# The first block's transitions of a fused transformer kernel: four weight tiles of the next stage are multiplied with the unnormalized residual sum, and the layer norm is applied to the products

## Chip, cores and metric

The kernel runs on one core of one Trainium2 chip. The metric is the device time of one execution in microseconds; lower is better. Three timed runs and one profiled execution of the kernel before are shown.

## What is computed

The input is one sequence of 256 tokens with 1024 features, in float32. The first block has two layers (the second block follows and is not touched). In each layer a mixer (sparse attention in layer 0, differential attention in layer 1) and a squared-ReLU MLP of 4096 hidden units are added to the stream through a layer norm:

```python
for l in range(DEPTH):
    sh1, sc1, g1, sh2, sc2, g2 = split(c_act @ ada_w[l] + ada_b[l], 6)
    y = mixer(modulate(x, sh1, sc1))
    x = layer_norm(ALPHA * x + (1 + g1) * y, ln_g[l, 0], ln_b[l, 0])
    y = sq_relu_mlp(modulate(x, sh2, sc2))
    x = layer_norm(ALPHA * x + (1 + g2) * y, ln_g[l, 1], ln_b[l, 1])
# modulate(x, shift, scale) = x * (1 + scale) + shift
```

A layer norm followed by `modulate` is `(r - mu) * rs * a + b` for each token, with a mean `mu` and an inverse deviation `rs` per token and a scale `a` and a shift `b` per feature. A following projection with weights `W` is therefore `rs * (W.(a*r) - mu * W.a) + W.b`: the product with the unnormalized `a*r` can be made before `mu` and `rs` are known.

## The kernel before

Activations lie with features on the partitions and the 256 tokens along the row, as eight tiles of 128x256. Every number that is multiplied is split into a high half in the reduced float32 format of TensorE (`fp32r`) and a low half, the rest; `mm3` (L385) makes three matmuls of 128x128 by 128x256 for each product: high by high, high by low, low by high. The stream is in `xa`, the modulated input of the next stage in `hh` (high halves) and `hl` (low halves).

All weights come from memory as tiles of 128x1024, 512 KB each (`load_raw`, L333, on the SP queue, whose order is that of the program). ScalarE makes the high half (`cast_hi`, L346, or L365 in `fetch`), VectorE or GpSimd the low half (`cast_lo`, L349, or L366). One tile of `up` or of a projection is 24 matmuls into one PSUM bank, one tile of `down` is 24 matmuls that add to eight output tiles `y` in four banks.

A transition is `tail` (L702) with `ln_finish` (L613) and `mod_apply` (L653). `tail` takes the last weight tiles of the stage that ends (`held`), loads the first eight tiles of the stage that follows (`following`), casts the first four of them, and finishes the output tiles one by one in the order 0, 2, 4, 6, 1, 3, 5, 7. For each, `tile_` (L626) adds gate times output to the stream (L633, VectorE), squares it (L635, ScalarE) and adds up sums and squares (L548: VectorE and GpSimd); narrow matmuls with ones make the column sums (L543). `rstd_rows` (L578) makes mean and variance on VectorE, the power of -0.5 on GpSimd (L591), and broadcasts both along the partitions into PSUM by eight small matmuls (L575). `warm` (L596) puts matmuls with zeros between. Then `apply` (L665) goes through the eight tiles: subtract the mean (L669), scale (L673), high half with the shift (L609, ScalarE), low half (L611). After the loop come the residual updates for the next transition (L515).

The transitions that the diff touches:

- Transition 1, `rest0` (L1505): the output projection of layer 0 into the first MLP. Right after it `late_loads` (L1914) loads the constants of the later stages, behind a GpSimd copy (L437) that reads the last tile of `hh`.
- Transition 2, the end of the first `mlp` (L833) into layer 1, `mix1` (L1532). The work list there is `ORDER1` (L33): eight value tiles, then `q` and `k` of eight heads; `queue1` (L1589) starts a head of attention when the values and its `q` and `k` are there. VectorE, ScalarE and GpSimd work in the program's order there.
- Transition 3, `rest1` (L1687): the output projection of layer 1 into the second MLP. Before that MLP two GpSimd operations (L1702, L1703) make a copy of the second block's meta tokens.

The stage that follows transitions 1 and 3 begins with `mlp_head` (L820): the first four `up` tiles, with the tiles' eight row slices outermost, so that it can start when the first tile of `hh` is there. In `mlp` the dot products of later modulation vectors (`ada`, L491: a 512 KB load and one VectorE operation each) and then the residual updates are spread over the loop by `tick` (L511).

Outside of regions marked `manual_schedule` (SP everywhere; TensorE in `tail`, by the last entry of `MAN`, L38), a scheduler fixes each engine's order when the program is built: among what is ready in its own estimate, what comes first in the program. `fenced` (L371) keeps weight casts on ScalarE and VectorE behind the last operations of `apply` on the same engine.

## Time and profile before

| | |
|---|---|
| median of three runs | 1179.38 us (1176.38 to 1181.78) |
| profiled execution | 1184.45 us |
| its span, first to last instruction | 1182.7 us |
| granted TensorE clock, mean | 0.942 |
| transition 1, 2, 3: last down matmul ends at | 219.87, 411.70, 555.67 us |
| first matmul with the new `hh` | 226.19, 418.76, 569.17 us |

Times inside the profiled execution count from the start of its span. A line of the timeline gives the start, the duration, the engine, the line of the program, the operation, the tile written and the tiles read, how many were merged, and in brackets how long the engine was idle before and what ended that. Matmuls overlap, so a duration of 0.28 us stands for a step of about 0.12 us from start to start.

### The profile page before, as it was taken

The numbers are of one execution on the slowest core, as the hardware profiler recorded it, in microseconds if no ns is written. First come the engines' busy times: TensorE is split into PE (matmuls) and PEld (weight loads), VectorE is DVE, ScalarE is ACT, GpSimd is POOL, SyncE is SP. The second block draws the span as 40 slices with busy tenths as digits, with TensorE's granted clock in tenths as the row PEclk, the third lists the DMA queues.
The fourth block names the chain that finished last, engine by engine and source line by source line (L and its number), as shares of the span: only waits on it lengthen the run. The fifth ranks groups of instructions, "written<-read, shape, count | busy, mean of one in ns | idle before, by whom it ended". The sixth has DMA issues, their size and how long they took to land.

```text
span 1182.7 us, 20550 instructions
## 1 busy us (share of the span) xinstructions
PE 1088.2 (92%) x7766; PEld 989.8 (84%) x7766; DVE 836.4 (71%) x1656; ACT 603.8 (51%) x1256; POOL 313.5 (27%) x343
## 2 busy tenths in 40 slices
PE   2889989999999999887999999998799989999997
PEld 1768667999999978777999999897786888899996
DVE  7575986799886577766886555579996667755553
ACT  2455757464445456554654444467445353644442
POOL 3283563200000208665000000417654350000000
PEclk9786998999999989898899999899999997999999
DMA  9966642299996238446387554022211151756520
GB/s 344 313 253 208 250 166 82 104 388 345 340 334 230 90 114 279 146 159 232 118 309 251 189 185 140 12 86 93 73 54 37 72 193 45 267 191 184 190 90 36
DMA packets 60448, 212.59 MB, mean 180 GB/s; under 512 B 6619, under 2 KB 9084, under 8 KB 60348
## 3 DMA queue, kind: packets, MB, share of 16 engines
q1 hardware_dynamic: 59424, 209.43, 50.9%
q0 software_dynamic: 192, 0.79, 0.4%
q8 instruction: 61, 1.00, 0.4%
q10 hardware_dynamic: 732, 1.05, 0.3%
q14 instruction: 39, 0.32, 0.1%
HBM read 209.15 MB, written 1.84 MB: 178 GB/s over the span
## 4 chain that ended last, share of the span: by engine, by line
PE 69%; DVE 13%; DMA 5%; POOL 5%; issue 4%; ACT 3%; SPq 0%; POOLq 0%; DVEq 0%; ACTq 0%
PE y L387 10%; PE y L388 10%; PE y L389 10%; PE pj L387 7%; PE pj L388 7%; PE pj L389 7%; PE tr L392 3%; DMA raw<-in_ws 3%; PE y L401 2%; DVE lo L352 2%; PE y L392 1%; PE pj L392 1%; DVE cva L2176 1%; PE cm L392 1%; DVE raw L478 1%
## 5 line engine op out<-in xcount | busy, mean ns | idle before, releaser
L366 DVE TENSOR_TENSOR lo<-raw,hi 128x1024 fp32r<-128x1024 f32 (+1 forms) x208 | 226.8, 1106 | 107.0 <-ACT hi L365 106.9
L365 ACT ACTIVATE hi<-raw 128x1024 fp32r<-128x1024 f32 (+1 forms) x208 | 195.3, 958 | 94.7 <-PE pj L388 77.0
L387 PE MATMUL pj<-hh,hi 128*128 128x256 f32 x768 | 217.1, 283 | 0.3
L388 PE MATMUL pj<-hl,hi 128*128 128x256 f32 x768 | 216.6, 282 | 0.3 <-DVE hl L1749 0.3
L389 PE MATMUL pj<-hh,lo 128*128 128x256 f32 x768 | 215.7, 281 | 0.0
L352 POOL TENSOR_TENSOR lo<-raw,hi 128x512 fp32r<-128x512 f32 (+3 forms) x48 | 75.4, 1577 | 360.6 <-ACT hi L347 355.1
L352 DVE TENSOR_TENSOR lo<-raw,hi 128x1024 fp32r<-128x1024 f32 (+2 forms) x103 | 124.0, 1211 | 41.8 <-ACT hi L347 40.5
L387 PEld LDWEIGHTS pj<-hh,hi 128*128 128x128 f32 x768 | 145.1, 189 | 2.7 <-ACT relu L807 0.9
L388 PEld LDWEIGHTS pj<-hl,hi 128*128 128x128 f32 x768 | 145.1, 189 | 2.0 <-DVE hl L1749 0.5
L388 PE MATMUL y<-actl,hi 128*128 128x256 f32 x512 | 144.3, 282 | 1.3 <-DVE actl L810 1.2
L389 PEld LDWEIGHTS pj<-hh,lo 128*128 128x128 f32 x768 | 145.3, 189 | 0.0
L387 PE MATMUL y<-acth,hi 128*128 128x256 f32 x512 | 144.1, 281 | 0.0
L389 PE MATMUL y<-acth,lo 128*128 128x256 f32 x512 | 143.7, 281 | 0.0
L347 ACT ACTIVATE hi<-raw 128x1024 fp32r<-128x1024 f32 (+2 forms) x107 | 110.7, 1042 | 24.1 <-DMA raw<-in_ws 13.7
L388 PEld LDWEIGHTS y<-actl,hi 128*128 128x128 f32 x512 | 97.0, 189 | 1.9 <-DVE actl L810 1.9
L387 PEld LDWEIGHTS y<-acth,hi 128*128 128x128 f32 x512 | 97.1, 190 | 0.1
L389 PEld LDWEIGHTS y<-acth,lo 128*128 128x128 f32 x512 | 96.8, 189 | 0.0
L478 DVE CUSTOM_DVE_ANT_0 raw<-raw,cact 128x1024 f32<-128x1024 f32 x67 | 86.6, 1301 | 3.3 <-DMA raw<-in_ws 3.1
L388 PE MATMUL y<-hl,hi 128*128 128x256 f32 x296 | 86.6, 293 | 0.0
L387 PE MATMUL y<-hh,hi 128*128 128x256 f32 x264 | 81.5, 309 | 2.2 <-ACT f L1586 2.2
L809 ACT ACTIVATE acth<-act 128x256 fp32r<-128x256 f32 x96 | 39.4, 416 | 83.5 <-DVE act L808 83.5
L389 PE MATMUL y<-hh,lo 128*128 128x256 f32 x264 | 77.9, 295 | 0.0
(658 smaller groups left out, 2556.9 us busy)
## 6 DMA issues: line engine op xcount, KB each, us to landing
raw<-in_ws SPq DMA_DIRECT2D x372, 512.0 KB, 4.7
bm<-bscr SPq DMA_DIRECT2D x4, 512.0 KB, 14.2
raw<-in_ws SPq DMA_DIRECT2D x4, 416.0 KB, 8.8
bm<-in_ws SPq DMA_DIRECT2D x3, 512.0 KB, 8.5
raw<-in_ws SPq DMA_DIRECT2D x3, 408.0 KB, 3.8
zn<-in_ws SPq DMA_DIRECT2D x2, 512.0 KB, 6.9
xa<-in_xT SPq DMA_DIRECT2D x2, 512.0 KB, 6.9
oh<-in_ws SPq DMA_DIRECT2D x2, 512.0 KB, 7.8
```

The lines of the kernel that those rows point to most:

```text
L347: return self.nc.scalar.activation(w[1], w[0], AF.Copy)
L352: return eng.tensor_tensor(w[2][:, a:b], w[0][:, a:b], w[1][:, a:b].bitcast(F32), op=OP.subtract)
L365: i = nc.scalar.activation(hi[:, a:b], raw[:, a:b], AF.Copy)
L366: j = (lo_by or nc.vector).tensor_tensor(lo[:, a:b], raw[:, a:b], hi[:, a:b].bitcast(F32), op=OP.subtract)
L387: mm(out, lh, rh, start=start, stop=False, skip_group_check=True)
L388: mm(out, lh, rl, start=False, stop=False, skip_group_check=True)
L389: mm(out, ll, rh, start=False, stop=stop, skip_group_check=True)
L392: self.nc.tensor.matmul(out, l, r, start=start, stop=stop, skip_group_check=True)
L401: last = self.nc.tensor.matmul(out, l, r, start=start, stop=stop, skip_group_check=True)
L478: nc.vector.tensor_tensor_reduce(out=raw, in0=raw, in1=self.cact, op0=OP.mult, op1=OP.add, scale=0.5, scalar=0.0, accum_out=t)
L809: nc.scalar.activation(ah, f, AF.Copy)
L2176: nc.vector.scalar_tensor_tensor(a, x[:, i:i + 272], w[:, j, i:i + 1], a, op0=OP.mult, op1=OP.add)
```

## The change

In the three transitions the first four weight tiles that follow (the head) are multiplied with `a*r`, whose high and low halves go into `hh` and `hl` as the output tiles are finished (`raw`). Two more columns, 256 and 257, hold `a` and `b`, so the same matmuls (258 columns) also make `W.a` and `W.b`. The head takes the two `pj` banks and `y0` and `y1`; its eight steps are put between the column sums and the broadcasts of mean and scale, whose rows now go to `y2` and `y3`; the fillers are gone there. `apply` still makes the normalized `hh` and `hl`, in the order `KS`, in the place of the raw ones, for the later weight tiles. Each head is read out of PSUM by `head_value`: two columns copied by ScalarE, `mu * W.a - product` and a multiplication by `rs` on VectorE; then `head_act` (activation of the MLP) or `head_qk` (scaled copy). The first is placed in the sixth step of the loop, three behind it.

In transition 2 the head is q0, k0, q1, k1, which `ORDER1` no longer has, and the eight tiles loaded ahead are these and v0 to v3. In the MLPs a fifth and sixth tile (`up4`, `dn0`) are cast in the transition, their low halves on GpSimd, the fourth tile's low half moves to GpSimd too, GpSimd is put into the program's order in `tail`, the downs of the first four tiles follow one by one between the next ups, and the meta-token copies are emitted among the dot products of the second MLP.

```diff
-ORDER1 = """v0 v1 v2 v3 v4 v5 v6 v7 q0 k0 q1 k1 q2 k2 q3 k3 q4 k4 q5 k5 q6 k6 q7 k7"""
+ORDER1 = """v0 v1 v2 v3 v4 v5 v6 v7 q2 k2 q3 k3 q4 k4 q5 k5 q6 k6 q7 k7"""
...
+            if head:
+                c.mod.raw(m, r[m])
             if n == 7:
                 c.one[1]()
                 c.two[1]()
-                self.warm(2)
+                if head:
+                    next(head)
+                else:
+                    self.warm(2)
                 c.one[1]()
                 c.two[1]()
...
+            st = self.ln_stats(c.s)
+            next(head)
+            mu = self.rows_of(st[:, 0:2], "y2")
             next(work, None)
-            c.mod(c.r, mu, rs, work)
+            next(head)
+            rs = self.rows_of(st[:, 2:4], "y3")
+            for _ in head:
+                pass
+            c.mod.apply(c.r, mu, rs, work, evict)
...
+        def raw(m, r):
+            hh, hl = self.hh[:, m, 0:256], self.hl[:, m, 0:256]
+            nc.scalar.activation(hh, r, AF.Copy, scale=c.a[:, m:m + 1])
+            nc.vector.scalar_tensor_tensor(hl, r, c.a[:, m:m + 1], hh.bitcast(F32), op0=OP.mult, op1=OP.subtract)
...
+            for n in range(10):
+                if n < 8:
+                    m = KS[n]
+                    nc.vector.tensor_sub(r[m], r[m], mu)
+                if n == 1:
+                    nc.scalar.activation(rows, rs, AF.Copy)
+                    nc.scalar.activation(mus, mu, AF.Copy)
+                if 1 <= n < 9:
+                    k = KS[n - 1]
...
+                if n == 5:
+                    evict(0, mus, rows)
+            self.fence = [self.fence_, lo()]
+            for j in range(1, 4):
+                evict(j, mus, rows)
...
+    def raw_head(self, ws):
+        ps = self.heads = [self.PS(t) for t in ("pj", "pj", "y0", "y1")]
+        for n, k in enumerate(KS):
+            sl = slice(128 * k, 128 * k + 128)
+            for p, (wh, wl) in zip(ps, ws):
+                self.mm3(p[:, :258], wh[:, sl], wl[:, sl], self.hh[:, k, 0:258], self.hl[:, k, 0:258], n == 0, n == 7)
+            yield
+
+    def head_value(self, j, mu, rs):
+        nc = self.nc
+        p = self.heads[j]
+        ab = self.T(self.small, (128, 2), "headab", bufs=4)
+        nc.scalar.activation(ab, p[:, 256:258], AF.Copy)
+        t = self.T(self.lnp, (128, 256), "full", bufs=3)
+        nc.vector.scalar_tensor_tensor(t, mu, ab[:, 0:1], p[:, 0:256], op0=OP.mult, op1=OP.subtract)
+        nc.vector.tensor_mul(t, t, rs)
+        return t, ab[:, 1:2]
...
-        with self.ordered(MAN[4]):
+        with self.ordered("PG" if evict else MAN[4]):
...
+            if evict:
+                self.cast_lo(nx[2], nc.vector)
+                self.cast_hi(nx[3])
+                self.cast_lo(nx[3], nc.gpsimd)
 
             def work():
+                if evict:
+                    for n in following[4:6]:
+                        w = self.arrive(n)
+                        self.cast_hi(w)
+                        more.append(w)
+                    yield
+                    for w in more:
+                        self.cast_lo(w, nc.gpsimd)
+                    yield
+                    return
...
+    def head_act(self, j, mu, rs):
+        t, b = self.head_value(j, mu, rs)
+        self.pend.append((j, self.mlp_act(t, scale=-1.0, bias=b)))
...
-        return [f"up{l}_{j}" for j in range(5)] + [f"dn{l}_{j}" for j in range(3)]
+        return [f"up{l}_{j}" for j in range(5)] + [f"dn{l}_0"] + ([f"up{l}_5", f"dn{l}_1"] if l < 2 else
+                                                              [f"dn{l}_1", f"dn{l}_2"])
...
-        n = 8 * len(vectors) + 8
+        self.fill = self.chain(*(self.ada(*lv) for lv in vectors), more, self.fill)
+        n = 8 * len(vectors) + 10
...
-            while len(pend) > 1 and pend[0][0] < 29:
+            while len(pend) > (4 if j < 8 else 1) and pend[0][0] < 29:
...
-            with self.fenced():
-                nc.gpsimd.tensor_copy(mh, meta)
-                nc.gpsimd.tensor_tensor(ml, meta, mh.bitcast(F32), op=OP.subtract)
...
+    def meta_eight(self):
+        nc = self.nc
+        self.mrep = [self.T(self.acts, (128, 8, 128), tag, F32R) for tag in ("oh", "ol")]
+        mh, ml = (t.rearrange("p k (e t) -> p k e t", e=8) for t in self.mrep)
+        meta = self.metaT[:, :, None, :].to_broadcast([128, 8, 8, 16])
+        nc.gpsimd.tensor_copy(mh, meta)
+        yield
+        nc.gpsimd.tensor_tensor(ml, meta, mh.bitcast(F32), op=OP.subtract)
```

## Rows read from the trace of the kernel before

**Rows 1.** Part 4 of the page: the chain that ended last, shares of the span by engine.

```profile
PE 69%; DVE 13%; DMA 5%; POOL 5%; issue 4%; ACT 3%; SPq 0%; POOLq 0%; DVEq 0%; ACTq 0%
```

**Rows 2.** Windows: stretch, busy us of five engines, clock, DMA share, GB/s.

```profile
219.87:226.19 6.32, 6.31 (x37) 4.66 (x35) 2.93 (x10) 0.93 (x2) 1.23 (x2) 0.73 0.01 4
411.70:418.76 7.06, 6.86 (x33) 4.91 (x32) 3.24 (x11) 1.22 (x3) 1.26 (x2) 0.63 0.00 0
555.67:569.17 13.50, 8.62 (x33) 6.45 (x33) 7.98 (x14) 1.22 (x3) 6.47 (x5) 0.50 0.24 91
242.62:400.00 157.38, 157.38 (x1330) 157.38 (x1331) 128.26 (x196) 79.12 (x122) 2.40 (x1) 1.00 0.85 310
```

**Rows 3.** Timeline of transition 1, all engines; the last row from TensorE's own timeline.

```profile
220.07 0.48 DVE L633 SCALAR_TENSOR_TENSOR zn<-y,mod,xa 128x256 f32<-128x256 f32 x1 [0.43 <-PE y L389]
...
222.32 0.16 DVE L585 TENSOR_SCALAR st<-tr 128x2 f32<-128x2 f32 x1 [1.76 <-PE tr L392]
...
222.53 2.41 PE L392 MATMUL y<-p_first,st 128*128 128x128 f32 x8
...
222.95 0.72 POOL L591 TENSOR_TENSOR st<-va,mhalf 128x2 f32<-128x2 f32 x1 [2.57 <-DVE va L587]
...
224.98 0.48 DVE L673 SCALAR_TENSOR_TENSOR full<-zn,acol,y 128x256 f32<-128x256 f32 x1 [0.37 <-PE y L392]
...
226.19 0.47 PE L387 MATMUL pj<-hh,hi 128*128 128x256 f32 x1
...
242.62 0.39 PE L388 MATMUL y<-actl,hi 128*128 128x256 f32 x1 [1.21 <-DVE actl L810]
```

**Rows 4.** Windows: the head of the first MLP, four up tiles.

```profile
226.19:237.81 11.62, 11.62 (x97) 11.34 (x96) 11.44 (x27) 7.80 (x17) 0.50 (x2) 1.00 0.25 86
```

**Rows 5.** Timeline of VectorE in transition 1: one step of the loop.

```profile
228.74 0.41 DVE L669 TENSOR_TENSOR zn<-zn,y 128x256 f32<-128x256 f32 x1
229.07 0.47 DVE L673 SCALAR_TENSOR_TENSOR full<-zn,acol,y 128x256 f32<-128x256 f32 x1
229.46 0.48 DVE L611 SCALAR_TENSOR_TENSOR hl<-full,bcol,hh 128x256 fp32r<-128x256 f32 x1
229.86 0.41 DVE L669 TENSOR_TENSOR zn<-zn,y 128x256 f32<-128x256 f32 x1
```

**Rows 6.** Timeline of VectorE and GpSimd ahead of transition 1: casts alone and together.

```profile
206.45 1.22 DVE L352 TENSOR_TENSOR lo<-raw,hi 128x1024 fp32r<-128x1024 f32 x1
...
207.51 2.44 POOL L352 TENSOR_TENSOR lo<-raw,hi 128x1024 fp32r<-128x1024 f32 x1 [13.05 <-ACT hi L347]
...
208.85 2.19 DVE L352 TENSOR_TENSOR lo<-raw,hi 128x1024 fp32r<-128x1024 f32 x1 [1.18 <-ACT hi L347]
```

**Rows 7.** Timeline of GpSimd and SP behind transition 1; landing of the transfer issued at 236.49.

```profile
233.17 0.18 POOL L437 COPY p_late<-hh 128x1 f32<-128x1 f32 x1 [9.51 <-ACT hh L609]
...
236.49 0.87 SPq L336 DMA_DIRECT2D raw<-in_ws  x2
...
DMA to landing us min/median/max: 11.1/11.1/11.1
```

**Rows 8.** Windows: values of layer 1; its first four projections; the other twelve.

```profile
418.76:442.30 23.54, 23.54 (x100) 18.87 (x99) 17.97 (x34) 14.06 (x25) 0.00 (x0) 0.96 0.36 122
442.30:454.70 12.40, 12.40 (x106) 11.93 (x105) 9.35 (x19) 8.58 (x20) 12.08 (x8) 1.00 0.91 335
454.70:521.00 66.30, 56.72 (x422) 50.51 (x420) 47.75 (x113) 41.50 (x123) 48.69 (x42) 0.92 0.59 197
```

**Rows 9.** Timeline of GpSimd and TensorE in transition 3.

```profile
555.75 1.04 POOL L1702 CAST oh<-metaT 128x1024 fp32r<-128x1024 f32 x1 [1.98 <-PE y L389]
...
557.61 2.77 POOL L1703 TENSOR_TENSOR ol<-metaT,oh 128x1024 fp32r<-128x1024 f32 x1
...
561.56 1.01 PE L392 MATMUL tr<-ones,run 128*128 128x1 f32 x4 [3.44 <-POOL run L559]
```

**Rows 10.** Timeline of VectorE behind the loop of transition 1.

```profile
233.56 0.87 DVE L519 SCALAR_TENSOR_TENSOR xa<-zn,lnalpha,hfull 128x256 f32<-128x256 f32 x2
```

More of the change, by code (lines that the diff above doesn't have):

```diff
@@ L23 @@
 W2 = 4
+KS = (0, 2, 4, 6, 1, 3, 5, 7)
 UNIT = 2
@@ L653, in mod_apply @@
     def mod_apply(self, li, sc, sh):
         nc = self.nc
+        c = SimpleNamespace()
         def begin():
             sc1, shift = self.need(*sc), self.need(*sh)
-            a = self.T(self.small, (128, 8), "acol", bufs=2)
-            b = self.T(self.small, (128, 8), "bcol", bufs=2)
-            nc.vector.tensor_mul(a, sc1, self.lncol[:, 2 * li, :])
-            nc.vector.tensor_mul(b, sc1, self.lncol[:, 2 * li + 1, :])
-            nc.vector.tensor_add(b, b, shift)
-            def apply(r, mu, rs, work):
-                lo = None
-                for m in range(10):
-                    if m < 8:
-                        nc.vector.tensor_sub(r[m], r[m], mu)
-                    if 1 <= m < 9:
-                        k = m - 1
-                        full = self.T(self.lnp, (128, 256), "full", bufs=3)
-                        nc.vector.scalar_tensor_tensor(full, r[k], a[:, k:k + 1], rs, op0=OP.mult, op1=OP.mult)
-                        if lo:
-                            lo()
-                        lo = self.put(k, full, b[:, k:k + 1])
-                    if m == 2:
-                        next(work, None)
-                self.fence = [self.fence_, lo()]
-                rows = self.T(self.resid, (128, 1024), "hfull", bufs=1)[:, :256]
-                nc.scalar.activation(rows, rs, AF.Copy)
-                self.fill = self.residual(li, r, rows)
@@ new lines, in apply @@
+        def apply(r, mu, rs, work, evict):
+            rows = self.T(self.resid, (128, 1024), "hfull", bufs=1)
+            rows, mus = rows[:, 0:256], rows[:, 256:512]
+            lo = None
+            for n in range(10):
[7 more added lines that the diff above has]
+                    k = KS[n - 1]
+                    full = self.T(self.lnp, (128, 256), "full", bufs=3)
+                    nc.vector.scalar_tensor_tensor(full, r[k], c.a[:, k:k + 1], rs, op0=OP.mult, op1=OP.mult)
+                    if lo:
+                        lo()
+                    lo = self.put(k, full, c.b[:, k:k + 1])
+                if n == 2:
+                    next(work, None)
+                if n == 5:
[3 more added lines that the diff above has]
+                evict(j, mus, rows)
+            self.fill = self.residual(li, r, rows)
@@ L714, in tail @@
             acts = before()
-            self.idle = self.PS("pj")
+            if not evict:
+                self.idle = self.PS("pj")
             if acts is not None:
@@ L729, in work @@
                     yield
-            for n, m in enumerate((0, 2, 4, 6, 1, 3, 5, 7)):
+            head = (self.raw_head([w[1:] for w in nx]),) if evict else ()
+            for n, m in enumerate(KS):
                 if m > 3:
@@ L737, in tail @@
                 self.down(y, m, (wh, wl), *a, last=True)
-                finish[1](n, m, y[m])
-                if n == 3:
+                finish[1](n, m, y[m], *head)
+                if n == 3 and not evict:
                     for w in nx[3:]:
@@ L742, in tail @@
             k = work()
-            self.warm(1)
-            finish[2](k)
+            if not evict:
+                self.warm(1)
+            finish[2](k, *head, *((evict,) if evict else ()))
             for _ in k:
                 pass
-        for n, w in zip(following, nx):
+        if evict:
+            nx = []
+        for n, w in [*zip(following, nx), *zip(following[4:], more)]:
             self.done[n] = w[1], w[2]
@@ L797, in out_proj, with mlp_act @@
         finish[0]()
-        self.tail(self.y, [(f"{name}{k}", halves(k)) for k in order], finish, following)
+        self.tail(self.y, [(f"{name}{k}", halves(k)) for k in order], finish, following, evict=evict)
         self.y = []
-    def mlp_act(self, p):
+    def mlp_act(self, p, **affine):
         nc = self.nc
```

94 lines of the change are left out of this document (62 added, 32 removed).

## Prediction

> **What bounds the kernel now.** I read the page first: TensorE holds 69% of the chain that ended last and VectorE 13% [rows 1], so time can be won where TensorE waits or does filler, and VectorE is the next to bind. Then the windows around the three places that the diff touches, from the end of the last down matmul to the first useful matmul of what follows: 6.32 us (transition 1, into the first MLP), 7.06 us (transition 2, into layer 1) and 13.50 us (transition 3, into the second MLP) [rows 2]. TensorE reads as busy there, but on zeros, sums and row broadcasts, at 0.50 to 0.73 of its clock. The last row of the group shows what stands behind transition 1: 157.38 of 157.38 us busy, so what is won before it stays won unless weights come late. The timeline of transition 1 says what fills the gap: last residual sum 220.07, statistics 222.32, power on GpSimd until 223.67, row broadcasts from 222.53, first scaled tile 224.98, head 226.19; and one more stall of 1.21 us at 242.62 [rows 3]. All three gaps together are 26.9 us.
>
> **The change, part by part.** The head (four weight tiles in eight slices each, 96 matmuls) no longer waits for the statistics. It took 11.62 us [rows 4]: 0.121 us for a matmul, 1.45 us for each of its eight k steps, 2.9 us for a weight tile of 24 matmuls; 258 columns for 256 add under 0.1 us. Removed: 8 filler matmuls per transition, off the path once real work stands there. Added on VectorE: 8 low halves of the raw sum before the statistics, and per head one correction and one multiply. One step of the normalizing loop, 1.12 us, is a subtraction (0.33 us from start to start), a scaling (0.39) and a low half (0.40) [rows 5]. So 8 x 0.40 = 3.2 us are added before the statistics and 4 x (0.40 + 0.33) = 2.9 us behind the head. Off VectorE go the casts of one to three weights (1.22 us each [rows 6]), to GpSimd. ScalarE gets 8 high halves, four copies of two columns and a row copy; it waits for VectorE through these stretches, so I cost it at nothing; without that cover it is 8 x 0.5 us.
>
> **Transition 1.** VectorE was idle before the last sum and before the statistics [rows 3], so of the 3.2 us I put 1.0 us on the path: statistics at 223.3. TensorE meanwhile does k step 1, then the sums, k step 2, the mean rows, k step 3, the scale rows, in an order that is fixed: subtraction from about 225.6, scaling from 227.9, head done at 235.0 (219.87 + 8 x 1.45 + 3.5: the eight row broadcasts took 2.41 us at about half the clock [rows 2, 3], so 1.2; the narrow sums, which lay between 220.07 and 222.32, I estimate at 1.2; 1.1 for one wait for VectorE). The loop's subtractions are done early, so 8 x 0.79 us end at about 235.5, held at the end by the head, which still reads what is overwritten. The evictions follow, one bank each 0.73 us; up-tile 4 needs the first bank and runs 236.0 to 238.9, and the downs need all four banks and the first activation: 239.0 against 242.62 [rows 3]. That is 3.6 us won.
>
> It is given back by the weights. The constants and all later loads wait on SP behind a GpSimd copy of the last normalized tile (233.17); the up-tile issued as the seventh transfer, at 236.49, landed 11.1 us later, at 247.6 [rows 7], 14.4 us after that copy. Now the copy comes at about 235.9, and the seventh transfer is up-tile 6: landed 250.3, cast 251.4. TensorE, which does up 4 before 239.0 and then down 0, up 5 and down 1, wants it at 239.0 + 3 x 2.9 = 247.7 and gets it at 251.4; before, it had done the same number of tiles at 242.6 + 3 x 2.9 = 251.3. Sum for transition 1: 0. Bounds: 3.6 us gain if the weights are in time, 4 us loss if the loop ends 4 us later.
>
> **Transition 2.** By the same sum the head (q0, k0, q1, k1) ends 15.1 us after the last down (411.7): 426.8. The values need the head's banks, evicted in order, so I start them at 428.3; they took 23.54 us at a clock of 0.96, some of it low, so 22.6: 450.9. Before, values and these four projections were done at 454.7 [rows 8]: 3.8 us won. What follows (454.7 to 521: 56.7 of 66.3 us busy [rows 8]) waits between heads of attention. The first scores now start about 2 us later, the second and third earlier. I add nothing for that; bounds 3 us loss to 10 us gain, since these waits move with the order on four engines. The transfers are the same eight, in another order.
>
> **Transition 3.** Here two GpSimd operations of the next stage, 1.04 and 2.77 us, ran between the sums of squares, and TensorE waited 3.44 us for the last one [rows 9]. The change emits them later, inside the MLP; but it also puts a weight cast of some 2.4 us ahead of the sums on the same engine [rows 6]. I let the head start at 557.5 (last down 555.67), give it 11.6 us, 3.5 us for sums, rows and a wait, 2 us for the clock, which was 0.50 through this gap [rows 2], and 2 us for GpSimd: done at 576.6 against about 581.2 (569.17 + 11.6 and a first part at half clock), 4.6 us won, less 1 us for the evictions in front of the downs: 3.6 us. No constants are loaded here, and weights can start early, since two of them are cast at once. Bounds: 0 to 10 us.
>
> **Sum.** 0 + 3.8 + 3.6 = 7.4 us off the profiled execution of 1184.45 us (span 1182.7): 1177.0. That execution lies 5.1 us above the median of the runs, 1179.38; against the median the forecast is 1172.0 us.
>
> **Rivals.**
> (a) The gaps come back in full: weights in time in transition 1 (3.6), attention of layer 1 moving ahead with its first heads (8), transition 3 down to the pattern of transition 1 (10, its bound): 21.6 us, 1158. For it: TensorE is never without work that is ready. Against: every evicted bank and every overwritten tile goes through VectorE, already without a gap in the loop [rows 5].
> (b) It moves and doesn't shrink, or the change doesn't do what it says: the scheduler pulls the two GpSimd operations forward again. That it does such things is in the trace: a residual update that is emitted behind 32 dot products of the MLP ran at 233.56, right behind the loop [rows 10]. The weights bind in transition 1, the banks in transition 2: about 1179, within 2 us.
> (c) Slower: VectorE and GpSimd shut each other out. Place: GpSimd's casts behind the power (two more, 2.44 us each), beside the loop's and the raw sum's low halves. Rows: a cast that takes VectorE 1.22 us took 2.19 us beside one of 2.44 us on GpSimd and ended 1.1 us after it [rows 6]. Price: up to 4.9 us in each transition, with 3.2 and 2.9 us of new work all on the path: 11 us against the 6.3 and 7.1 us of gaps 1 and 2, and level in gap 3; that is 4.7 + 3.9 = 8.6 us slower, 1188. It decides from the point where the loop ends more than about 3 us later than the head. Against it: the casts beside the loop are two per transition, and only low halves were seen to stop beside one. The Trainium skill, page SBUF — State Buffer, section Who interferes with whom, states it as a rule: a VectorE instruction with two inputs in SBUF and a GpSimd instruction that reads SBUF exclude each other for the whole instruction. By that rule (the trace agrees in this pair) subtraction and scaling, which read one input from PSUM, go on, about half of the 4.9 us is lost in each of the three transitions, and the sum would be about 1179 instead of 1172.
>
> **Numbers.** A measurement of this kernel can tell about 0.5%, 5.9 us, from no change. Forecast (gain of 4 to 11 us) 0.50; (a) 0.12; (b) 0.22; (c) 0.16. Faster by over 5.9 us: (a) and most of the forecast, 0.43, together 0.55. Same: (b) and the rest of the forecast, 0.29. Slower: (c), 0.16. The forecast's own range is 1168 to 1176. With 2 in 10 left out, the lower half of (a) and the upper part of (c), the range is 1159 to 1185.
>
> **What would show it.** Right: matmuls of 258 columns directly behind the last down in all three transitions at full clock; in transition 1 a stall of TensorE for up-tile 6 near 248; the values' start near 428 held by an eviction; no wait for a sum of squares over 1 us in transition 3. Wrong: no such stall and the MLP running 3 us earlier; VectorE low halves of over 1 us beside GpSimd casts; the two GpSimd operations again in front of the power; attention of layer 1 ending more than 8 us earlier or later against the values' end. If any one transition loses more than 3 us, or layer 1's attention shifts by 8, the forecast falls.

## The result and the profile after

The changed kernel takes 1213.15 us (median of four runs, 1209.84 to 1215.45) against 1178.1 us of the kernel before: ratio 1.0291, 95% interval 1.0255 to 1.0327. The forecast was 1172, with a range of 1159 to 1185: wrong in sign. The profiled execution has a span of 1213.7 us (before 1182.7).

To see where 31 us went, I took the starts of the first residual sums (`zn<-y,mod,xa`, one row per transition in the view of the tile `zn`) as marks. The row has the shortest, median and longest of eight operations in ns, then the start of the first and of the last.

```profile
L635 DVE SCALAR_TENSOR_TENSOR zn<-y,mod,xa x8: 468/472/485, 211.5 to 217.7; 128x256 f32<-128x256 f32 x8
L635 DVE SCALAR_TENSOR_TENSOR zn<-y,mod,xa x8: 469/476/485, 419.4 to 425.6; 128x256 f32<-128x256 f32 x8
L635 DVE SCALAR_TENSOR_TENSOR zn<-y,mod,xa x8: 470/473/477, 570.2 to 586.9; 128x256 f32<-128x256 f32 x8
L635 DVE SCALAR_TENSOR_TENSOR zn<-y,mod,xa x8: 472/481/484, 770.3 to 776.6; 128x256 f32<-128x256 f32 x8
```

From mark to mark come four stretches and a rest; T4 is the last transition of the first block, which the change leaves alone. All runs of this study, in us (median of the timed runs; ratio to the kernel before; then the stretches of the profiled execution):

| run | median | ratio, interval | to T1 | T1 to T2 | T2 to T3 | T3 to T4 | rest |
|---|---|---|---|---|---|---|---|
| before | 1178.1 | | 214.1 | 191.4 | 141.4 | 200.4 | 435.4 |
| **after** | 1213.15 | 1.0291 (1.0255-1.0327) | 211.5 | 207.9 | 150.8 | 200.1 | 443.4 |
| t1_only | 1191.44 | 1.0123 (1.0085-1.0162) | 207.6 | 206.2 | 140.3 | 200.2 | 433.1 |
| t2_only | 1191.37 | 1.0148 (1.0082-1.0214) | 207.9 | 192.3 | 147.8 | 200.7 | 438.3 |
| t3_only | 1181.40 | 1.0038 (1.0011-1.0065) | 208.0 | 191.6 | 142.2 | 201.8 | 436.2 |
| rr_bank | 1211.40 | 1.0300 (1.0249-1.0351) | 208.3 | 207.7 | 150.4 | 200.3 | 441.0 |
| steps_first | 1197.05 | 1.0160 (1.0109-1.0211) | 207.7 | 202.9 | 140.5 | 203.7 | 437.2 |
| fillers | 1205.04 | 1.0225 (1.0201-1.0249) | 209.3 | 204.5 | 143.9 | 203.4 | 443.1 |
| no_raw_low | 1205.36 | 1.0225 (1.0197-1.0254) | 209.4 | 204.2 | 146.8 | 201.5 | 443.4 |
| gate_first | 1210.17 | 1.0269 (1.0226-1.0313) | 210.3 | 203.5 | 151.3 | 200.4 | 443.3 |
| ticks_late | 1200.25 | 1.0188 (1.0134-1.0241) | 205.4 | 197.6 | 146.8 | 203.3 | 444.2 |
| before_ticks | 1178.75 | 0.9991 (0.9973-1.0009) | 209.5 | 191.1 | 141.3 | 200.4 | 435.3 |
| casts_off | 1218.91 | 1.0351 (1.0300-1.0402) | 207.1 | 203.8 | 154.7 | 210.3 | 439.3 |
| meta_after | 1210.71 | 1.0281 (1.0250-1.0312) | 210.8 | 207.8 | 150.3 | 201.7 | 442.2 |
| all_five | 1184.18 | 1.0054 (1.0025-1.0084) | 208.6 | 192.5 | 142.8 | 199.0 | 437.6 |
| two_three | 1184.17 | 1.0065 (1.0035-1.0095) | - | - | - | - | - |
| five_no_low | 1180.99 | 1.0027 (0.9999-1.0055) | 207.2 | 192.2 | 140.9 | 201.0 | 437.9 |
| four_mends | 1184.80 | 1.0043 (1.0014-1.0073) | 210.3 | 192.2 | 143.2 | 200.0 | 436.4 |
| six_mends | 1181.68 | 1.0026 (1.0007-1.0045) | 207.4 | 190.5 | 143.8 | 198.8 | 434.7 |

The profiled execution of two_three lay 16 us above its median, so its stretches are left out. The first column, where no kernel differs in the work, spreads over 9 us, the rest over some 3 us in kernels that have the same code there: smaller differences in one execution are not read.

After against before: -2.6, +16.5, +9.4, -0.3, +8.0, together the 31.0 us. So transition 1 with its MLP loses most, transition 2 next, transition 3 nothing; and 8 us are lost in the second block, which the diff doesn't touch.

**Transition 1, the statistics.** Timelines of VectorE, of TensorE and of GpSimd in the changed kernel:

```profile
217.72 0.47 DVE L635 SCALAR_TENSOR_TENSOR zn<-y,mod,xa 128x256 f32<-128x256 f32 x1
218.11 1.89 DVE L702 SCALAR_TENSOR_TENSOR hl<-zn,abcol,hh 128x256 fp32r<-128x256 f32 x2
219.92 0.41 DVE L561 TENSOR_TENSOR run<-run,zn 128x256 f32<-128x256 f32 x1
220.26 0.87 DVE L702 SCALAR_TENSOR_TENSOR hl<-zn,abcol,hh 128x256 fp32r<-128x256 f32 x2
226.58 0.16 DVE L677 TENSOR_SCALAR st<-tr 128x2 f32<-128x2 f32 x1 [5.45 <-PE tr L394]
229.99 0.75 DVE L711 TENSOR_TENSOR zn<-zn,y 128x256 f32<-128x256 f32 x2 [2.86 <-PE y L394]
...
220.39 1.87 PE L394 MATMUL tr<-ones,run 128*128 128x1 f32 x8 [2.61 <-DVE run L561]
222.12 0.56 PE L389 MATMUL pj<-hh,hi 128*128 128x258 f32 x1
...
224.84 0.85 PE L394 MATMUL tr<-ones,zn 128*128 128x1 f32 x4
...
218.12 0.73 POOL L558 TENSOR_TENSOR run<-sq,sq 128x256 f32<-128x256 f32 x1 [1.73 <-ACT sq L637]
218.93 0.79 POOL L561 TENSOR_TENSOR run<-run,sq 128x256 f32<-128x256 f32 x1
```

Two raw low halves stand ahead of the last running sum on VectorE and take 1.89 us; running sums of squares run on GpSimd beside them (218.12 to 219.72). The next two, with GpSimd idle, take 0.87 us. TensorE, whose order is fixed, waits 2.61 us for that sum; then its clock is at half, and the head's first step takes 2.7 us (222.12 to 224.84), not 1.45. The statistics come 8.9 us after the last residual sum (217.72 to 226.58); before, 2.25 [rows 3]. The windows show what that does to VectorE; five after and five before, in the same places counted from the transition (columns as in [rows 2]: behind the length of the stretch stand the busy times of PE, PEld and VectorE):

```profile
217.78:222.78 5.00, 2.39 (x11) 2.39 (x12) 3.35 (x7) 3.02 (x7) 1.51 (x2) 0.65 0.02 5
222.78:227.78 5.00, 5.00 (x25) 5.00 (x25) 0.48 (x3) 0.00 (x0) 0.57 (x1) 0.50 0.00 0
227.78:232.78 5.00, 5.00 (x37) 5.00 (x36) 2.28 (x7) 0.77 (x2) 4.83 (x3) 0.82 0.00 0
247.78:252.78 5.00, 2.43 (x19) 2.02 (x17) 4.59 (x10) 0.85 (x4) 1.52 (x2) 1.00 1.03 416
252.78:257.78 5.00, 3.42 (x14) 3.12 (x15) 5.00 (x11) 1.83 (x4) 0.00 (x0) 0.57 1.04 404
```

```profile
219.87:224.87 5.00, 4.99 (x32) 4.21 (x31) 1.72 (x6) 0.42 (x1) 1.23 (x2) 0.76 0.01 3
224.87:229.87 5.00, 5.00 (x34) 3.84 (x33) 4.89 (x14) 2.33 (x5) 0.00 (x0) 0.90 0.01 2
229.87:234.87 5.00, 5.00 (x44) 5.00 (x44) 4.82 (x13) 3.50 (x9) 0.50 (x2) 1.00 0.09 18
249.87:254.87 5.00, 5.00 (x46) 5.00 (x45) 5.00 (x10) 1.80 (x4) 0.00 (x0) 1.00 1.03 419
254.87:259.87 5.00, 5.00 (x45) 5.00 (x44) 5.00 (x10) 4.14 (x8) 0.00 (x0) 1.00 1.03 415
```

In the first 15 us VectorE works 6.11 us after and 11.43 us before: 5.3 us of it are lost waiting for statistics, while it has more to do. TensorE pays 30 us later. **The stall in the MLP**, VectorE, TensorE and ScalarE:

```profile
250.37 0.68 DVE L368 TENSOR_TENSOR lo<-raw,hi 128x512 fp32r<-128x512 f32 x1
250.97 1.22 DVE L480 CUSTOM_DVE_ANT_0 raw<-raw,cact 128x1024 f32<-128x1024 f32 x1
252.12 1.23 DVE L480 CUSTOM_DVE_ANT_0 raw<-raw,cact 128x1024 f32<-128x1024 f32 x1
...
251.11 0.39 PE L391 MATMUL pj<-hh,lo 128*128 128x256 f32 x1 [2.34 <-DVE lo L368]
...
254.35 0.58 PE L391 MATMUL y<-acth,lo 128*128 128x256 f32 x1 [1.79 <-DVE lo L368]
...
241.40 2.18 ACT L367 ACTIVATE hi<-raw 128x512 fp32r<-128x512 f32 x4
```

The weights lay in SBUF (ScalarE made their high halves from 241.4 to 243.6); the four low halves that belong to them are made at 245.35, 250.37, 253.61 and 255.70. The second stands on VectorE behind the loop, the evictions and the late constants (1.02 us of it an idle wait for their transfer), the third behind two dot products more (L480).

**Transition 2** has the same picture (first row), and ahead of it a new shut-out: an activation's square on VectorE takes 2.49 us beside the fourth tile's cast on GpSimd (415.13 to 417.57). **Transition 3**: the two copies of the meta tokens still run between the sums of squares (the three POOL rows). **Block 2** begins with a wait for a PSUM bank:

```profile
428.31 1.87 PE L394 MATMUL tr<-ones,run 128*128 128x1 f32 x8 [2.72 <-DVE run L561]
...
415.35 2.49 DVE L895 TENSOR_TENSOR act<-relu 128x256 f32<-128x256 f32 x1 [0.80 <-ACT relu L894]
...
582.18 1.23 POOL L1812 CAST oh<-metaT 128x1024 fp32r<-128x1024 f32 x1 [2.26 <-PE y L391]
583.49 2.39 POOL L1814 TENSOR_TENSOR ol<-metaT,oh 128x1024 fp32r<-128x1024 f32 x1
585.84 0.90 POOL L558 TENSOR_TENSOR run<-sq,sq 128x256 f32<-128x256 f32 x1
...
797.43 0.57 PE L389 MATMUL a<-hi,oh 128*128 128x272 f32 x1 [2.17 <-DVE full L1887]
```

### The profile page after: what moved, and what is told of

It is laid out like the page before. It is cut to its first block, busy times and chain, and to the rows that moved or that the text cites. A ratio compares the mean times of both kernels' runs of the same rounds, so it can differ in the third digit from the quotient of the medians.

```text
span 1213.7 us, 20617 instructions
## 1 busy us (share of the span) xinstructions
PE 1095.1 (90%) x7742; PEld 999.9 (82%) x7742; DVE 852.5 (70%) x1697; ACT 618.0 (51%) x1298; POOL 333.1 (27%) x350
## 4 chain that ended last, share of the span: by engine, by line
PE 65%; DVE 16%; DMA 5%; issue 5%; POOL 4%; ACT 4%; POOLq 0%; DVEq 0%; SPq 0%; ACTq 0%
PE y L389 10%; PE y L391 10%; PE y L390 9%; PE pj L389 7%; PE pj L391 7%; PE pj L390 7%; PE tr L394 3%; DVE lo L354 3%; DMA raw<-in_ws 3%; PE y L403 2%; DVE raw L480 1%; PE y L394 1%; DVE cva L2284 1%; PE d L394 1%; POOL se L1557 1%
## 5 line engine op out<-in xcount | busy, mean ns | idle before, releaser
L368 DVE TENSOR_TENSOR lo<-raw,hi 128x1024 fp32r<-128x1024 f32 (+1 forms) x204 | 221.3, 1102 | 101.1 <-ACT hi L367 100.8
L367 ACT ACTIVATE hi<-raw 128x1024 fp32r<-128x1024 f32 (+1 forms) x204 | 190.6, 955 | 89.3 <-PE pj L390 70.3
L391 PE MATMUL pj<-hh,lo 128*128 128x256 f32 (+1 forms) x752 | 214.2, 285 | 4.5 <-DVE lo L368 4.5
L389 PE MATMUL pj<-hh,hi 128*128 128x256 f32 (+1 forms) x752 | 215.5, 287 | 0.2 <-ACT hh L1856 0.2
L390 PE MATMUL pj<-hl,hi 128*128 128x256 f32 (+1 forms) x752 | 214.9, 286 | 0.7 <-DVE hl L613 0.3
L354 POOL TENSOR_TENSOR lo<-raw,hi 128x512 fp32r<-128x512 f32 (+3 forms) x55 | 94.6, 1727 | 390.7 <-ACT hi L349 377.2
L354 DVE TENSOR_TENSOR lo<-raw,hi 128x1024 fp32r<-128x1024 f32 (+2 forms) x95 | 119.0, 1259 | 49.2 <-ACT hi L349 46.6
L349 ACT ACTIVATE hi<-raw 128x1024 fp32r<-128x1024 f32 (+2 forms) x111 | 115.0, 1042 | 36.0 <-DMA raw<-in_ws 15.1
L390 PE MATMUL y<-hl,hi 128*128 128x256 f32 (+1 forms) x312 | 90.6, 291 | 0.0
L389 PE MATMUL y<-hh,hi 128*128 128x256 f32 (+1 forms) x280 | 85.8, 307 | 3.4 <-ACT f L1688 1.8
L480 DVE CUSTOM_DVE_ANT_0 raw<-raw,cact 128x1024 f32<-128x1024 f32 x67 | 86.3, 1292 | 3.4 <-DMA raw<-in_ws 3.4
L391 PE MATMUL y<-hh,lo 128*128 128x256 f32 (+1 forms) x280 | 82.7, 295 | 0.0
```

Of the source, the lines that this page charges most:

```text
L349: return self.nc.scalar.activation(w[1], w[0], AF.Copy)
L354: return eng.tensor_tensor(w[2][:, a:b], w[0][:, a:b], w[1][:, a:b].bitcast(F32), op=OP.subtract)
L367: i = nc.scalar.activation(hi[:, a:b], raw[:, a:b], AF.Copy)
L368: j = (lo_by or nc.vector).tensor_tensor(lo[:, a:b], raw[:, a:b], hi[:, a:b].bitcast(F32), op=OP.subtract)
L389: mm(out, lh, rh, start=start, stop=False, skip_group_check=True)
L390: mm(out, lh, rl, start=False, stop=False, skip_group_check=True)
```

## Experiments

### One transition at a time

Edit: for the transitions left as before, the old functions are called (`mod_apply`, `mlp_first`, `mlp_head`, `ORDER1` and the place of the meta copies of the kernel before).

> Only transition 1 is changed; transitions 2 and 3 are those of the kernel before. From the two traces: the changed kernel's first residual sum of transition 2 comes 13.8 us later than before although transition 1 began 2.6 us earlier, so transition 1 and the MLP behind it lose 16.4 us by themselves. Theory A (each transition loses for itself): about 13 to 16 us slower than before (1191 to 1194), and in block 2 no further loss. Rival (one shared cause, the shift of the weight stream after transition 1, makes all the losses): the whole 31 us, 1209.

> Only transition 2 is changed. Theory A: 9.5 us lost between the first residual sums of transitions 2 and 3, and 4.7 us at the start of block 2, where the first product that goes into bank a has to wait 2.2 us for the last normalizing product of VectorE, which reads the rows from the same physical bank in the changed program and from another one in the program before; together 14 us slower (1192), 17 if the half clock near 901 us comes with it. Rival (shared cause): within 3 us of before, 1178.

> Only transition 3 and the two GpSimd copies of the meta tokens are changed. Theory A: level with before (0.3 us faster in the changed kernel's trace), 1178, and no wait for bank a at the start of block 2. Rival 1 (its gain is eaten by the late state that the earlier transitions leave): 3 to 4 us faster, 1175, as predicted. Rival 2 (the loss in block 2 belongs to the moved copies): 8 us slower, 1186.

Measured: +1.23%, +1.48%, +0.38%, together 3.1% against 2.9% for all three. Transitions 1 and 2 lose for themselves, and no shared cause carries the losses on; transition 3 alone is within 0.5% of level. Transition 2 alone also lengthens the start of block 2: from T4's first residual sum to block 2's first `xp` it is 39.1 us, with transition 1 alone 35.8, before 36.0, after 41.2.

### Order of TensorE, clock, and the raw low halves

```diff
             if n == 7:
+                if head:
+                    next(head)
+                    next(head)
                 c.one[1]()
                 c.two[1]()
-                if head:
-                    next(head)
-                else:
+                if not head:
                     self.warm(2)
```

> The changed kernel with another order on TensorE: the head's first two steps stand ahead of the column sums of the last tiles, instead of one step between them. In the changed kernel TensorE waits 2.61 us for a running sum that VectorE makes behind two low halves of the raw sum, its clock falls to half, and the statistics come 8.8 us after the last down matmul (before: 2.5). Theory A (this late start is the larger part of transition 1's loss): no wait over 1 us there, statistics 3 to 5 us earlier in all three transitions, 6 to 12 us faster than the changed kernel, 1202 to 1207. Rival V (VectorE's own amount of work sets the end, whenever the statistics come): under 3 us faster.

Measured: 16 us faster than after. In transitions 1 and 2 there is no wait and a clock of 1.00; the statistics come 4.7 us after the last residual sum (213.9 to 218.59 in transition 1). T1 to T2 gives back 5.0 us, T2 to T3 10.3, all that transition 2 had lost. Not so in transition 3: TensorE waits 3.53 us for a residual sum, its clock is 0.50 before and behind that wait, and T3 to T4 is 3.6 us longer. Theory A holds for transitions 1 and 2, and more of the time hangs on this order than I gave it. Windows of transition 1 from the last residual sum:

```profile
213.90:215.90 2.00, 2.00 (x19) 2.00 (x18) 2.00 (x4) 2.00 (x7) 1.51 (x2) 1.00 0.03 8
215.90:217.90 2.00, 2.00 (x20) 1.93 (x18) 1.44 (x4) 1.10 (x2) 0.03 (x1) 1.00 0.01 4
217.90:219.90 2.00, 2.00 (x18) 2.00 (x19) 0.48 (x3) 0.00 (x0) 0.68 (x1) 1.00 0.00 0
```

Is it the wait or the clock? One run puts ten fillers (matmuls with zeros) into the wait; another leaves out the low halves of the raw sum:

```diff
             if n == 7:
+                if head:
+                    self.idle = self.PS("tr")
+                    self.warm(10)
                 c.one[1]()
...
             nc.scalar.activation(hh, r, AF.Copy, scale=c.a[:, m:m + 1])
-            nc.vector.scalar_tensor_tensor(hl, r, c.a[:, m:m + 1], hh.bitcast(F32), op0=OP.mult, op1=OP.subtract)
```

> The changed kernel with ten matmuls on zeros in TensorE's 2.6 us wait for the running sum, in all three transitions. Theory C (the half clock that follows the wait is what costs, since the head's first steps run at it): granted clock 0.9 or more from 218 to 228, head's first step 1.45 us instead of 2.8, statistics 2 to 4 us earlier per transition, 6 to 10 us faster than the changed kernel, 1203 to 1207. Theory O (the order of VectorE's work costs; the clock is a by-product): the running sum ends when it did, statistics at most 1 us earlier, 1211 to 1214.

> The changed kernel without the eight low halves of the raw sum (the low part of the raw sum is left out of the head's products, which read what is there; the matmuls are the same). Theory: these eight operations hold up the running sum; without them TensorE's wait is under 0.5 us, the statistics come 3.5 us after the last down matmul as the prediction had it, and 8 to 14 us go in transitions 1 and 2, 1199 to 1205. Rival (the wait comes from GpSimd's sums of squares or from ScalarE's high halves): under 3 us faster.

Measured: 8.1 us faster with fillers, though the running sum ended when it did: theory C. In transitions 1 and 2 the clock is 1.00 throughout (in transition 3 it still falls to 0.50), the statistics of transition 1 come 6.1 us behind the last sum (215.6 to 221.66); T2 to T3 gets 6.9 of its 9.4 us back. Without the low halves the run is 7.8 us faster, just short of the 8 to 14 expected: the wait is gone, as the theory said, the statistics still come 5.2 us behind, and the half clock is still there, with TensorE never idle:

```profile
213.60:215.60 2.00, 2.00 (x20) 1.99 (x19) 1.88 (x5) 2.00 (x7) 1.32 (x3) 1.00 0.00 0
215.60:217.60 2.00, 2.00 (x15) 1.94 (x15) 0.47 (x1) 2.00 (x4) 0.52 (x1) 0.86 0.03 8
217.60:219.60 2.00, 2.00 (x12) 2.00 (x11) 0.00 (x0) 0.56 (x1) 0.00 (x0) 0.50 0.00 0
219.60:221.60 2.00, 2.00 (x10) 2.00 (x10) 0.48 (x3) 0.00 (x0) 0.18 (x1) 0.50 0.00 0
...
214.14 0.95 PE L394 MATMUL tr<-ones,run 128*128 128x1 f32 x8
214.94 0.36 PE L389 MATMUL y<-oh,hi 128*128 128x256 f32 x1
...
215.59 1.19 PE L394 MATMUL tr<-ones,run 128*128 128x1 f32 x8
216.64 0.37 PE L389 MATMUL pj<-hh,hi 128*128 128x258 f32 x1
```

Two groups of eight one-column matmuls stand there with three wide matmuls (and two of four columns) between them. In steps_first 24 more wide matmuls (two steps of the head) stand between these groups, in the run with fillers ten fillers, and the clock stays. The kernel before has the two groups with the same three wide matmuls between them, and two of its fillers behind the second:

```profile
219.43 0.36 PE L387 MATMUL y<-oh,hi 128*128 128x256 f32 x1
...
220.01 1.03 PE L392 MATMUL tr<-ones,run 128*128 128x1 f32 x8
220.90 0.59 PE L392 MATMUL pj<-zero 128*128 128x512 bf16 x2
221.33 0.50 PE L392 MATMUL tr<-ones,zn 128*128 128x1 f32 x4
```

There too the clock fell behind them: 1.00 from 219.87 to 221.87, 0.64 in the next 2 us, 0.50 in the 2 us after that. What ran at half clock there was the row broadcasts and fillers; in the changed kernel it is the first two steps of the head, with the last sums between them.

### Weights or VectorE in the first MLP

```diff
-            self.late_loads(late, self.hh[:, 7, 0:1].bitcast(F32))
+            self.late_loads(late, self.hh[:, 0, 0:1].bitcast(F32))
```

```diff
-            self.tick(n * (j - 3) // 26 - n * (j - 4) // 26)
+            f = lambda i: max(n * (i - 9) // 20, 0) if l == 0 else n * (i - 3) // 26
+            self.tick(f(j) - f(j - 1))
```

The first edit is gate_first, the second ticks_late; before_ticks makes the second in the kernel before.

> The changed kernel; the late loads of transition 1 wait for the first normalized tile (about 232) instead of the last (241.6), so all weights behind them start some 9 us earlier. Theory W (the restarted stream of weights, as predicted, makes the stall of the first MLP at 248 to 254): the stall goes, 4 to 8 us faster than the changed kernel, 1205 to 1209. Theory V (the stall waits for casts that VectorE does late; the weights lay there): under 2 us faster, and TensorE still waits for low halves.

> The changed kernel; in the first MLP the dot products of the modulation vectors (a load and 1.15 us of VectorE each) and the residual updates begin five up tiles later. Theory V: VectorE's queue behind the loop shrinks by 4 dot products and 2 updates, 5.6 us, and TensorE's waits at 248 to 254 (4.1 us) go: 3 to 6 us faster, 1207 to 1210. Theory W: 1 to 2 us faster, since the up tile then lands four transfers earlier but the gate still opens at 241.6. Both would see nothing change in transitions 2 and 3.

> Control: the kernel before with the dot products and residual updates of the first MLP five up tiles later, as in the run that did this to the changed kernel. Theory V: in the kernel before VectorE caught up with its casts while TensorE did the head (3.69 us of low halves at 234.35), so nothing waits there and the time is level, 1177 to 1180. Rival (these dot products hold back any version, and the change has no part in it): 5 to 10 us faster, 1168 to 1173.

Measured: the gate opened at 232.09 instead of 241.56 and the first loads behind it went out 9.5 us earlier; the median is 3.0 us lower, inside the intervals, and T1 to T2 4.4 us shorter. The stall stayed, 4.49 us in one piece instead of 2.34 and 1.79. The order on VectorE in that run (three dot products, then the low halves), and TensorE's wait:

```profile
247.01 1.22 DVE L480 CUSTOM_DVE_ANT_0 raw<-raw,cact 128x1024 f32<-128x1024 f32 x1
...
250.09 1.22 DVE L480 CUSTOM_DVE_ANT_0 raw<-raw,cact 128x1024 f32<-128x1024 f32 x1
...
251.23 2.49 DVE L368 TENSOR_TENSOR lo<-raw,hi 128x512 fp32r<-128x512 f32 x4
...
251.97 0.48 PE L391 MATMUL pj<-hh,lo 128*128 128x256 f32 x1 [4.49 <-DVE lo L368]
```

Dot products later: 12.9 us faster, 10.3 of it in T1 to T2, more than twice what was expected: one wait of 2.32 us is left (the low half behind the late constants), the second is gone, and so is the half clock that followed (0.57 in the window from 252.78 above). Why T2 to T3 gained 4.0 us too is not settled. The control is plain: the same edit does nothing to the kernel before (0.9991). There VectorE made six low halves at 234.35, while TensorE did the head, so less was left to stand behind the dot products, and TensorE did not wait there:

```profile
234.35 3.69 DVE L366 TENSOR_TENSOR lo<-raw,hi 128x512 fp32r<-128x512 f32 x6
```

The restarted weights may cost some of it; the larger part is VectorE.

### GpSimd's casts

```diff
-                self.cast_lo(nx[3], nc.gpsimd)
+                self.cast_lo(nx[3], nc.vector)
...
                 if evict:
-                    for n in following[4:6]:
...
-                    yield
                     return
```

> The changed kernel without the casts that it moved to GpSimd: the low half of the fourth tile is made by VectorE, the fifth and sixth tile are cast behind the transition in the ordinary way. Theory L (the shut-out of VectorE by GpSimd, the prediction's rival c): 3 us faster in each transition, 1204 to 1208, and no VectorE operation of the raw sum over 1 us. Theory V (VectorE's work is the bound, and GpSimd's casts help): 1.2 us more VectorE work ahead of the statistics and 2.4 us behind, level to 6 us slower, 1213 to 1219.

Measured: 5.8 us slower than after, as theory V had it. In transition 1 the raw low halves took 0.47 to 0.57 us each, one of them 0.94, and T1 to T2 was 4.1 us shorter, so shut-outs probably cost there, though no run parts them from the rest of the edit; T2 to T3 and T3 to T4 were 3.9 and 10.2 us longer. On the whole the casts on GpSimd help (no run of either kernel reaches into the other's times, though the intervals of the ratios overlap): VectorE's work counts for more than what GpSimd shuts out. The prediction's rival (c) had the right engine and the wrong part of it.

### Meta copies and the bank of block 2

```diff
-        nc.gpsimd.tensor_copy(mh, meta)
+        with self.tc.issue_after(self.pow.ins):
+            nc.gpsimd.tensor_copy(mh, meta)
...
-            rr = self.rstd_rows(s, 1024)
+            rr = self.rstd_rows(s, 1024, tag="y0")
```

The first lines are from meta_after (`self.pow` is the power of the transition; the second copy is treated likewise), the last from rr_bank.

> The changed kernel; the two GpSimd copies of the meta tokens must follow the power of transition 3 on GpSimd. In the changed kernel they still run between the sums of squares of transition 3 (1.23 and 2.39 us in the run of transition 3 alone, where a running sum on VectorE beside the second took 2.55 us). Theory: TensorE's wait of 4.1 us for that running sum goes or shrinks to what raw low halves cost, 2 to 4 us faster than the changed kernel, 1209 to 1211, from transition 3 alone. Rival (VectorE's own raw low halves make the wait): under 1 us, 1213, with the wait still there.

> All three transitions changed, as in the changed kernel; the row broadcast of the last layer norm of block 1 goes to bank y0 instead of tr, so that the first product of block 2 into bank a finds a bank that nobody reads. Theory A: 4.7 us faster than the changed kernel (1208.5), 8 us (1205) if the half clock near 901 us follows from that wait. Rival (another operand is late there too): 1213, with a wait of 2 us for something else at the same matmul.

Measured: with the copies behind the power, TensorE's wait for the running sum fell from 4.11 to 2.19 us; ahead of it TensorE waits 5.66 us for residual sums, as in the changed kernel (1.94 and 3.51). T3 to T4 was 201.7 against 200.1, no gain, and the median is 2.4 us lower, inside the intervals. So the copies made part of one wait, and the rest is VectorE's own work, as the rival said, with a low half (2.58 us) and a cast (2.16 us) stretched beside GpSimd's casts in it. With the other bank the wait at the first `a` matmul is gone,

```profile
791.26 0.43 PE L389 MATMUL a<-hi,oh 128*128 128x272 f32 x1
```

and from T4 to the first `xp` it is 36.8 instead of 41.2 us: 4.4 of the 8 us of block 2. In the timed runs that is -1.8 us and lies inside the intervals, so the saving is shown in the trace alone. The other 3 us lie between block 2's first and last `xp` (98.3 to 103.3 us in the runs); what moves it is open.

### Mended versions

all_five has steps_first, gate_first, ticks_late, meta_after and rr_bank together; five_no_low leaves the raw low halves out of it; four_mends has no early gate; six_mends puts the work on the late constants into `with self.fenced():`, behind the loop. two_three has transition 1 of the kernel before, and steps_first, meta_after and rr_bank.

> The changed kernel with the five mends together: two head steps ahead of the column sums, late loads behind the first normalized tile, dot products of the first MLP later, the rows of the last layer norm in another bank, the meta copies behind the power. If the causes are separate, the parts add up: first to second transition 207.9 - 5.0 - 4.4 - 10.3 = 188 us, second to third 140.5, third to fourth 197 to 203, the rest 437: some 1177, within 5 us of the kernel before. Theory V (VectorE's amount of work in transition 1 remains the bound): the first stretch stays at 193 or more (before 191.4), 1180 to 1185. If the mends cure one and the same cause, 1190 to 1197.

> Transition 1 and the first MLP as in the kernel before; transitions 2 and 3 changed, with two head steps ahead of the column sums, the last rows in another bank and the meta copies behind the power. By the stretches of the mended runs: 191.4 + 140.5 + 199.0 against 191.4 + 141.4 + 200.4 of the kernel before, 2.3 us faster at best, 1176 to 1178, not to be told from the kernel before. If the change can pay outside transition 1 (the prediction's 3.8 and 3.6 us): 1171.

> The version with the five mends, again without the low halves of the raw sum, 8 operations or some 3.2 us of VectorE less per transition. Theory V (VectorE's work is what holds the mended version): 3 to 7 us faster than it, 1177 to 1181, the waits for the loop at 230 to 238 shorter. Rival (the evictions and the loop's own length, not the raw sum, hold it): 1182 to 1185, the same waits of 0.3 to 0.8 us for the last tiles.

> The version with the mends, without the early gate: the exponential of the late constants, which in the version with five mends held ScalarE for 2.00 us inside the loop, comes later, and so do the weights. If ScalarE's wait is what holds the mended version: first to second transition 190 to 191 us instead of 192.5, 1181 to 1183. If the weights matter more (4.4 us by the run with the early gate alone): 195 or more, 1187.

> The version with five mends, and the work on the late constants behind the last normalized tile on ScalarE and VectorE. If ScalarE's wait is the rest: no wait of ScalarE for p_rows inside the loop, first to second transition 190 us, 1180 to 1182, level with before. A version that beats the kernel before by more than 0.5% is not expected, since transition 2 and 3 in the mended runs are within 1.5 us of before. Rival (the loop with the evictions in it is itself too long): 192.5 again, 1184.

Measured: all_five gives back 29 of the 35 us of the medians. The stretch from T1 to T2 is 192.5: not the 188 that the parts add up to, so they overlap. Without the raw low halves it is 192.2, so their VectorE time isn't what is left there (the median is 3.2 us lower, inside the intervals). ScalarE's wait of 2.00 us for the constants inside the loop probably is: with that work behind the loop, in six_mends, the wait is gone and the stretch is 190.5, and the ratio 1.0026 in all (the intervals of the two overlap; the 2.0 us are read from one trace of each). four_mends gained nothing over all_five, so the early gate is worth what it cost there. No version is faster than the kernel before: six_mends and all_five are level with it by the bound of 0.5% or just over. two_three, expected to be level, is 0.65% slower; why is open.

## Why the prediction was wrong

**The step that failed first: "of the 3.2 us I put 1.0 us on the path: statistics at 223.3", 3.2 us after the last residual sum.** It was 8.9 us. Two terms were mis-sized. The raw low halves were counted as time on VectorE, not as work in front of the running sum for which TensorE's fixed order waits: 2.61 us, where the sum had 1.1 us for one wait. And the head's steps were costed at 1.45 us, the price at full clock, though they now stand where the granted clock of the kernel before was 0.73 in the mean [rows 2]; the first took 2.7 us. The narrow sums around it, estimated at 1.2 us, took 3.3 us at that clock. steps_first takes away the wait and the half clock in transitions 1 and 2 and is 16 us faster than after; fillers takes away the half clock alone and is 8 us faster.

**"Removed: 8 filler matmuls per transition, off the path once real work stands there."** That real work can stand there at full clock is what failed, and no run shows that these eight fillers would have kept the clock: with them in place the kernel before fell to 0.50 behind the same groups of narrow sums. What kept it at 1.00 in transitions 1 and 2 was wide matmuls or ten fillers between the two groups (steps_first, fillers); without these it falls even when TensorE never waits (no_raw_low).

**"It is given back by the weights", an up tile in transit.** The stall came where the prediction put it (248 to 254), but the weights lay there; VectorE's low halves were late. That the place was right is luck. The sum costed each operation and asked only for waits between loop and head. It did not ask what VectorE had done in the shadow of the head before, 3.69 us of casts, and what stood in its queue behind the loop now. The bound for transition 1, 4 us loss, was too narrow by 12.

**The loop "ends about 235.5".** From statistics to the last low half it took 15.5 us instead of the 12.2 that the working gives (223.3 to 235.5). Five more VectorE operations stand inside it, a residual update and the first eviction with its activation: 1.8 us by their starts. The rows of the mean come at half clock, 3.4 us behind the statistics instead of 2.3. Where the clock was at 1.00 it took 13.3 us (transition 2 of steps_first) and 14.0 (six_mends).

**Right, once the statistics are in time:** the head's length. In transition 2 of steps_first it runs from the last down matmul, 416.8, to 431.2: 14.4 us against 15.1 in the prediction. The first matmuls of the values come directly behind it; the next wait 2.60 us for an eviction, as forecast, and go on 17.8 us behind the last down matmul, where the forecast had 16.6:

```profile
431.06 0.50 PE L389 MATMUL c<-hi,hh 128*128 128x512 f32 x1
...
434.63 0.47 PE L389 MATMUL d<-hi,hh 128*128 128x512 f32 x1 [2.60 <-DVE full L751]
```

The 3.8 us for transition 2 shrink to 0.9 (141.4 to 140.5), no more than kernels with this transition unchanged differ among themselves (140.3 to 142.2).

**Transition 3, "3.6 us":** none. The meta copies were pulled forward again (rival b), and a running sum beside the second took 2.55 us. The eight residual sums took 16.8 us from first to last instead of 8.8: the raw low halves stand between them, one of them stretched to 2.58 us beside a cast on GpSimd; without them (no_raw_low) it was 11.7. The stretch comes out level, so the earlier head wins back no more than that.

**Rival (c)** named VectorE and the point from which it decides, a loop that ends more than 3 us behind the head; it ended at 242.1, the head at 239.1, so just at that point. Its mechanism is seen (1.89 us for two low halves, 2.49 for a square). The Trainium skill, page SBUF — State Buffer, section Who interferes with whom, excludes a VectorE operation with two inputs in SBUF and a GpSimd operation that reads SBUF from each other. These rows agree, while the residual sums, which read one input from PSUM, kept their 0.47 us. But taking the casts off GpSimd made the run 5.8 us slower, so these casts were not the price of the change.

**Not in the prediction at all:** 4.4 us in block 2, since with transition 2 changed the rows of the last layer norm came to lie in the PSUM bank that block 2 fills first.

## What to carry to other kernels

When work is moved ahead of a reduction, ask first what now stands in front of that reduction on every engine with a fixed order; an overlap that makes the statistics late loses more than it hides. Before an idle shadow is filled, list what other engines did in it (casts for the next stage, here) and where that goes. Before wide work is moved behind narrow matmuls and costed at full clock, look at the granted clock at that place; if it is low there, find an order with wide matmuls between the narrow ones.

## What was not expected of the hardware

The granted clock fell from 1.00 to 0.50 with TensorE 100% busy (no_raw_low, 215.6 to 221.6): what had run were 16 one-column matmuls with three wide ones and two of four columns between. It then stayed at half through two full steps of wide matmuls, the first of which took 2.4 us (216.64 to 219.05) instead of 1.45. With 24 wide matmuls or ten fillers more between the groups it did not fall in transitions 1 and 2 (steps_first, fillers). The kernel before shows the same fall, with TensorE busy too (1.99 of 2.00 us from 221.87 to 223.87), where it meets the broadcasts and fillers alone.
